# Two projection groups side by side, and smaller changes of order, loads and banks, in a hybrid attention block

## The chip, the cores and the metric

The kernel runs on one core of one Trainium2 chip. The metric is the device time of one execution in microseconds; the time before is the median of three runs.

## The reference

The block takes x (512 rows, 1024 columns, float32), normalises each row by its mean square, multiplies it by one wide input matrix, runs two attention branches of eight heads each on slices of the product, and merges them:

```python
h = rms_norm(x, norm_g)
proj = h @ w_in                      # 1024 x 6152
fq, fk, fv, fz, mq, mk, mv, mz, ga, gb, fl = split_cols(proj, IN_SPLITS)
log_f = log_sigmoid(fl + b_f)        # 8 columns
y_fox = fox_attention(rms_norm(fq), rms_norm(fk), fv, log_f) * silu(fz)
y_moba = moba_attention(rope(rms_norm(mq)), rope(rms_norm(mk)), mv) * silu(mz)
merged = sigmoid(ga + b0) * (y_fox @ w_fox) + sigmoid(gb + b1) * (y_moba @ w_moba)
out = x + merged @ w_out
```

## The kernel before, in words

Every product of two float32 matrices is made of three TensorE products of parts: each operand is split into a high part (a rounded copy) and a low part (what is left), and high x high, high x low and low x high are added up in PSUM. In the names, `wh_` and `wl_` are the parts of a weight, `Zh` and `Zl` those of x times norm_g (transposed, one tile of 128 x 512 for each of eight k), `Gh` and `Gl` those of the normalised x.

The matrix w_in is worked off in groups of 256 columns, named fqa, fka, fza and so on (a and b are the two halves of a slice). A group's weights come in two halves of four k each. The first two groups, fqa and fka (with the 8 columns of fl appended to fka), and the gates fza and fzb are multiplied by the parts Z, before the mean squares of the rows are known; later groups use G. `norm_row` turns the factors r of the rows into a tile (`rbc`) by four transposes on TensorE (tile `p_rbc`).

The start of the program: `first_loads` queues cst on ScalarE's queue and, on SyncE's, the pieces of fqa's weights (k 0, 1, 2 to 3, 4 to 7) between the eight tiles `xt` of x transposed. Eight products on a tile of zeros (`WARM`) run on TensorE meanwhile. `first_split` and `split_x` split what has landed; `load_fl` loads and splits fka's weights; `first_qk` multiplies all eight k of fqa into four PSUM banks (one for each 128 rows) and then all eight k of fka into the four others. `x_stats` loads x again by rows, in eight tiles of the tag "y" (15 buffers, eight of which hold `xt`), and sums the squares on ScalarE, with a scratch tile as output. `evac_qk` copies each bank to SBUF and normalises the heads.

Then come fza, fzb and fva, and four rounds of attention. `attn_group` gives the steps of a round of four heads: Tr (transposes and splits of q and k), Aa(h) (logits, minimum on VectorE, exponential on ScalarE), Bb(h) (transposes of the probabilities, products with v, sum into the tile `ypair`), Yp(pr) (product with the gate, split). The last step of a round, Yp(1), is run as `gate` inside the next round: before, behind that round's Aa(0). Projection groups are mixed in as filler. After that come the gate groups GA and GB, the products with w_moba, and the output product `group_o`, which makes a product of 2 x 2 blocks out of seven products of sums. `O_PRODUCTS` lists them with the number of the pair of PSUM banks that each is added into; `keep` copies banks to SBUF (`eo`) and adds x to them by a DMA from GpSimd, `result` adds a bank and a kept tile on VectorE (`ot`) and stores the sum.

PSUM has eight banks, in tags: "pj" 2, "tp" 3, "lg" 2, "pv" 1. The order of the instructions on each engine is set when the program is built, by a scheduler with modelled times that starts from the order of the text; on the chip each engine goes through its list in that order.

The order around the change, before:

```python
first_split(0, ((0,), (1, 2), (3, 4)))
first_split(1, ((5, 6), (7,)))
nc.sync.dma_start(out=wfl, in_=w_fl)
load_fl("fka", COLS["fka"], 0)
load_fl("fka", COLS["fka"], 1)
b1 = first_qk("fqa", (("pj", 2), ("pj", 2), ("lg", 2), ("lg", 2)))
b2 = first_qk("fka", (("tp", 3), ("tp", 3), ("tp", 3), ("pv", 1)))
```

Of the kernel before, what the change touches and what calls it, by code (L numbers as in the profile page):

```python
# [22 lines left out]
WARM = 8  # L23
# [6 lines left out]
def fox_moba_kernel(ctx: ExitStack, tc, xT, x, w_in, w_fl, w_fox, w_moba, w_out, cst, rope, out):  # L30
# [31 lines left out]

    XT, RAW = {}, {}

    def first_loads():
        def xt(eng, k):
            XT[k] = t2("y", 15, f"xt{k}")
            eng.dma_start(out=XT[k], in_=xT[:, k, :])

        def w(k0, k1):  # L70
            hf = k0 // 4
            if hf not in RAW:
                RAW[hf] = sb.tile([P, 4, CW], F32, name=f"wr_fqa{hf}", tag="wr", bufs=WR)
            nc.sync.dma_start(out=RAW[hf][:, k0 - 4 * hf:k1 - 4 * hf], in_=w_in[0, :, k0:k1, :])
# [46 lines left out]
    def split_x(*ks):  # L121
        for k in ks:
            xt = XT[k]
            zh, zl = Z[k] = [stage["pool"].tile([P, S], F32R, name=f"Z{hl}{k}") for hl in "hl"]
            A.activation(zh, xt, AF.Copy, scale=col(C_NG + k))
            V.scalar_tensor_tensor(zl, xt, col(C_NG + k), zh.bitcast(F32), op0=OP.mult, op1=OP.subtract)
# [12 lines left out]
    def load_fl(name, c0, hf):  # L139
        raw = sb.tile([P, 4, CW], F32, name=f"wr_{name}{hf}", tag="qk", bufs=4)  # L140
        nc.sync.dma_start(out=raw, in_=w_in[c0 // CW, :, 4 * hf:4 * hf + 4, :])
        hi, lo = split(raw, CW, f"{name}{hf}")
        f = wfl[:, 4 * hf:4 * hf + 4, :]
        A.activation(hi[:, :, CW:264], f, AF.Copy)
        V.tensor_tensor(out=lo[:, :, CW:264], in0=f, in1=hi[:, :, CW:264].bitcast(F32), op=OP.subtract)
        chunks.setdefault(name, []).append((hi, lo))

    def first_split(hf, between):
        raw = RAW[hf]
        hi = sb.tile([P, 4, 264], F32R, name=f"wh_fqa{hf}", tag="wh", bufs=4)  # L150
        lo = sb.tile([P, 4, 264], F32R, name=f"wl_fqa{hf}", tag="wl", bufs=4)
        for q, xs in enumerate(between):
            k = slice(2 * q, 2 * q + 2) if hf else slice(max(q, 2 * q - 2), max(q + 1, 2 * q))
            if hf == 0 and q < 2:
                V.tensor_copy(hi[:, k, :CW], raw[:, k])
            else:
                A.activation(hi[:, k, :CW], raw[:, k], AF.Copy)
            V.tensor_tensor(out=lo[:, k, :CW], in0=raw[:, k], in1=hi[:, k, :CW].bitcast(F32), op=OP.subtract)
            split_x(*xs)
        chunks.setdefault("fqa", []).append((hi, lo))  # L160

    COLS = {}
    off = 0
    for nm in ("fq", "fk", "fv", "fz", "mq", "mk", "mv", "mz"):
        for hfn in ("a", "b"):
            COLS[nm + hfn] = off
            off += CW
    for nm in ("ga", "gb"):
        for i in range(4):
            COLS[f"{nm}{i}"] = off  # L170
            off += CW
# [695 lines left out]
    def group_o():  # L867
# [74 lines left out]
        def keep(at, tq, cq):  # L942

            e[at] = sb.tile([P, 2, S], F32, name=f"eo{at}", tag="qk", bufs=4)
            for t in range(2):
                A.activation(e[at][:, t, :], b[at][t], AF.Copy)
                t0 = tq * HT + t * P
                G.dma_start(out=e[at][:, t, :], in_=x[t0:t0 + P, cq * 512:(cq + 1) * 512], accum_op=OP.add)
# [270 lines left out]
```

## Time and profile before

| | us |
|---|---|
| median of three runs | 426.72 (426.54 to 426.73) |
| the profiled execution, its own time | 427.16 |
| its span | 425.3 |
| TensorE busy | 418.5 |
| VectorE busy | 327.2 |
| ScalarE busy | 271.4 |
| GpSimd busy | 98.4 |

The span runs from the first to the last instruction of the profiled execution. A busy time counts an instruction's whole length. A line of the timeline gives start, length, engine, source line, operation, output and inputs; what stands in brackets is the idle time of that engine before it and what ended it.

### The profile page before, as it was taken

The numbers are of one execution on the slowest core, as the hardware profiler recorded it, in microseconds if no ns is written. First come the engines' busy times: TensorE is split into PE (matmuls) and PEld (weight loads), VectorE is DVE, ScalarE is ACT, GpSimd is POOL, SyncE is SP. The second block draws the span as 40 slices with busy tenths as digits, with TensorE's granted clock in tenths as the row PEclk, the third lists the DMA queues.
The fourth block names the chain that finished last, engine by engine and source line by source line (L and its number), as shares of the span: only waits on it lengthen the run. The fifth ranks groups of instructions, "written<-read, shape, count | busy, mean of one in ns | idle before, by whom it ended". The sixth has DMA issues, their size and how long they took to land.

```text
span 425.3 us, 7669 instructions
## 1 busy us (share of the span) xinstructions
PE 418.5 (98%) x2887; PEld 387.7 (91%) x2887; DVE 327.2 (77%) x570; ACT 271.4 (64%) x514; POOL 98.4 (23%) x120
## 2 busy tenths in 40 slices
PE   7999999999999999999999999999999999999996
PEld 6998899999999998899998878899999989988884
DVE  5669976769979769568767698767979698689973
ACT  4975436776868867568746687655656535686450
POOL 1048200225132850025750102140000000022140
PEclk9999999999999999999999999999999999999999
DMA  7981144235576334304124222463052603696484
GB/s 243 398 308 55 52 146 139 58 124 175 168 221 217 85 99 125 96 29 125 38 88 124 79 70 72 201 225 123 25 176 65 229 5 112 220 245 116 99 140 158
DMA packets 25621, 58.21 MB, mean 137 GB/s; under 512 B 3064, under 2 KB 7856, under 8 KB 25584
## 3 DMA queue, kind: packets, MB, share of 16 engines
q1 hardware_dynamic: 13392, 38.11, 27.3%
q10 hardware_dynamic: 8800, 11.21, 8.7%
q0 software_dynamic: 3392, 8.39, 8.5%
q8 instruction: 23, 0.38, 0.3%
q14 instruction: 14, 0.11, 0.1%
HBM read 48.11 MB, written 6.32 MB: 128 GB/s over the span
## 4 chain that ended last, share of the span: by engine, by line
PE 96%; DVE 2%; DMA 1%; issue 0%; ACT 0%; SPq 0%; DVEq 0%; ACTq 0%
PE pb_GB L753 3%; PE pb_GA L753 3%; PE pb_GB L750 3%; PE pb_GA L750 3%; PE pb_GB L752 3%; PE pb_GA L752 3%; PE po L939 3%; PE po L938 3%; PE po L940 3%; PE pv L611 2%; PE pv L610 2%; PE lg L556 2%; PE lg L555 2%; PE pm L681 2%; PE pm L680 2%; PE pm L679 2%
## 5 line engine op out<-in xcount | busy, mean ns | idle before, releaser
L560 ACT ACTIVATE p<-p,negm 128x128 f32<-128x128 f32 (+1 forms) x64 | 35.7, 559 | 9.8 <-DVE negm L558 8.6
L558 DVE CUSTOM_DVE_ANT_0 p<-lg,mask 128x128 f32<-128x128 f32 (+1 forms) x64 | 30.9, 485 | 14.3 <-PE lg L556 13.7
L334 POOL TENSOR_TENSOR ff<-ss,mh 128x8 f32<-128x8 f32 x16 | 26.7, 1678 | 65.2 <-DVE ss L332 64.7
L888 POOL DMA_DIRECT2D wr_o<-in_w_out_dram x4 | 4.9, 1293 | 95.5 <-ACT wr_o L887 95.5
L136 DVE TENSOR_TENSOR wl_GA<-wr_ga,wh_GA 128x1024 fp32r<-128x1024 f32 x14 | 17.8, 1288 | 5.8 <-ACT wh_GA L134 3.7
L901 ACT ACTIVATE wh_o<-wr_o 128x1024 fp32r<-128x1024 f32 x14 | 14.8, 1059 | 10.0 <-PE pb_GB L752 2.8
L134 ACT ACTIVATE wh_GB<-wr_gb 128x1024 fp32r<-128x1024 f32 x14 | 14.6, 1059 | 9.5 <-PE pm L680 3.5
L134 ACT ACTIVATE wh_GA<-wr_ga 128x1024 fp32r<-128x1024 f32 x14 | 14.6, 1059 | 9.3 <-PE pb_GA L752 4.6
L555 PE MATMUL lg<-KH,QS 128*128 128x128 f32 (+1 forms) x64 | 20.5, 329 | 0.0
L902 DVE TENSOR_TENSOR wl_o<-wr_o,wh_o 128x1024 fp32r<-128x1024 f32 x14 | 16.9, 1221 | 3.8 <-ACT wh_o L901 3.8
L136 DVE TENSOR_TENSOR wl_GB<-wr_gb,wh_GB 128x1024 fp32r<-128x1024 f32 x14 | 16.9, 1222 | 3.5 <-ACT wh_GB L134 3.5
L636 DVE TENSOR_TENSOR ypair<-pv,ysh 64x512 f32<-64x512 f32 x16 | 11.0, 688 | 11.0 <-ACT ysh L635 10.8
L607 DVE TENSOR_TENSOR ptl<-p_a,pth 128x512 fp32r<-128x512 f32 x16 | 11.0, 685 | 4.6 <-ACT pth L606 4.5
L529 DVE SCALAR_TENSOR_TENSOR QS<-p_qT,cs,QS 64x512 fp32r<-64x512 f32 x16 | 12.0, 750 | 2.5 <-ACT QS L528 2.1
L635 ACT ACTIVATE ysh<-pv 64x512 f32<-64x512 f32 x16 | 9.5, 593 | 6.7 <-PE pv L611 5.6
L753 PE MATMUL pb_GA<-Gh,wl_GA 128*128 128x256 f32 x48 | 13.6, 283 | 0.0
L752 PE MATMUL pb_GA<-Gl,wh_GA 128*128 128x256 f32 x48 | 13.5, 281 | 0.0
L750 PE MATMUL pb_GA<-Gh,wh_GA 128*128 128x256 f32 x48 | 13.5, 281 | 0.0
L753 PE MATMUL pb_GB<-Gh,wl_GB 128*128 128x256 f32 x48 | 13.5, 281 | 0.0
L752 PE MATMUL pb_GB<-Gl,wh_GB 128*128 128x256 f32 x48 | 13.4, 281 | 0.0
L679 PE MATMUL pf<-yhf,wh_wf 128*128 128x512 f32 x32 | 13.1, 408 | 0.4 <-DVE zs_mzb L425 0.4
L528 ACT ACTIVATE QS<-p_qT,cs 64x512 fp32r<-64x512 f32 x16 | 10.9, 681 | 3.8 <-PE lg L555 2.0
(458 smaller groups left out, 1785.9 us busy)
## 6 DMA issues: line engine op xcount, KB each, us to landing
wr_ga<-in_w_in_dram SPq DMA_DIRECT2D x8, 512.0 KB, 3.7
wr_gb<-in_w_in_dram SPq DMA_DIRECT2D x8, 512.0 KB, 5.1
wr_o<-in_w_out_dram SPq DMA_DIRECT2D x8, 512.0 KB, 5.1
xt<-in_xT_dram SPq DMA_DIRECT2D x8, 256.0 KB
x<-in_x_dram SPq DMA_DIRECT2D x8, 256.0 KB, 6.3
KH<-KH ACTq DMA_DIRECT2D x16, 128.0 KB, 2.4
s_dramh<-sum_sh ACTq DMA_DIRECT2D x8, 256.0 KB
s_draml<-sum_sl ACTq DMA_DIRECT2D x8, 256.0 KB, 3.6
```

The lines of the kernel that those rows point to most:

```text
L134: A.activation(hi[:, :, 0:n], src, AF.Copy)
L136: eng.tensor_tensor(out=lo[:, q, 0:n], in0=src[:, q], in1=hi[:, q, 0:n].bitcast(F32), op=OP.subtract)
L334: G.tensor_tensor(out=f2, in0=ss.rearrange("p t h -> p (t h)"), in1=mh, op=OP.pow)
L555: T.matmul(lg[:, :n], qs[:, qt], kh[:, :n], start=True, stop=False)
L558: V.tensor_tensor_reduce(pt, lg[:, :n], mask[:, 512 - n:512], -0.125, 3.0e38, op0=OP.add, op1=OP.min, accum_out=mkn[:, hh, i:i + 1])
L560: A.activation(pt, pt, AF.Exp, bias=mkn[:, hh, i:i + 1], scale=-1.0, accum_out=rs[:, hh, i:i + 1])
L679: T.matmul(p, hi[:, k, cc], yh, start=(k == 0), stop=False)
L750: T.matmul(o, hi[:, k, cc], lh, start=(n < 3 and c == 0 and k == 0), stop=False, skip_group_check=True)
L752: T.matmul(o, hi[:, k, cc], ll, start=False, stop=False, skip_group_check=True)
L753: T.matmul(o, lo[:, k, cc], lh, start=False, stop=(k == 3), skip_group_check=True)
L901: A.activation(wide(hi), wide(R[key, c]), AF.Copy)
L902: V.tensor_tensor(out=wide(lo), in0=wide(R[key, c]), in1=wide(hi).bitcast(F32), op=OP.subtract)
```

## The change

The first two groups are multiplied side by side: for each k first fqa's twelve products, then fka's, into all eight banks. The weights of fka are loaded in the same pieces as those of fqa, between the tiles of x, and `wfl` is loaded at the start on ScalarE's queue. The first tile of x comes in two halves, and is split in two halves. One warming product is left out. The last two tiles of `x_stats` get buffers of the tag "u", and the squares are written over their input. `norm_row` comes ahead of fka's evacuation. Yp(1) of a round stands behind Aa(1) of the next one. The second half of bank pair 3 is made in two quarters of 256 columns, the second one in a third bank of the tag "tp".

```diff
-WARM = 8
+WARM = 7
...
     def first_loads():
...
+        def w(nm, k0, k1):
             hf = k0 // 4
+            if (nm, hf) not in RAW:
+                tag, bufs = ("wr", WR) if nm == "fqa" else ("qk", 4)
+                RAW[nm, hf] = sb.tile([P, 4, CW], F32, name=f"wr_{nm}{hf}", tag=tag, bufs=bufs)
...
+        def xt(k, c0=0, c1=S):
+            if k not in XT:
+                XT[k] = t2("y", 15, f"xt{k}")
+            nc.sync.dma_start(out=XT[k][:, c0:c1], in_=xT[:, k, c0:c1])
         nc.scalar.dma_start(out=cs, in_=cst)
-        w(0, 1)
-        xt(nc.sync, 0)
-        w(1, 2)
-        xt(nc.sync, 1)
-        w(2, 4)
-        xt(nc.sync, 2)
-        xt(nc.sync, 3)
-        w(4, 8)
-        for k in range(4, KT):
-            xt(nc.sync, k)
+        nc.scalar.dma_start(out=wfl, in_=w_fl)
+        w("fqa", 0, 1)
+        xt(0, 0, 256)
+        xt(0, 256, S)
+        w("fka", 0, 1)
+        w("fqa", 1, 2)
+        xt(1)
+        w("fka", 1, 2)
+        w("fqa", 2, 4)
+        xt(2)
+        w("fka", 2, 4)
+        xt(3)
+        w("fqa", 4, 8)
+        xt(4)
+        w("fka", 4, 8)
+        for k in range(5, KT):
+            xt(k)
...
+    def split_x(k, parts=1):
+        xt = XT[k]
+        Z[k] = [stage["pool"].tile([P, S], F32R, name=f"Z{hl}{k}") for hl in "hl"]
+        n = S // parts
+        for c in (slice(i * n, (i + 1) * n) for i in range(parts)):
+            zh, zl = (z[:, c] for z in Z[k])
+            A.activation(zh, xt[:, c], AF.Copy, scale=col(C_NG + k))
+            V.scalar_tensor_tensor(zl, xt[:, c], col(C_NG + k), zh.bitcast(F32), op0=OP.mult, op1=OP.subtract)
...
+    def first_split(nm, k0, k1, on_v=False):
+        hf = k0 // 4
+        if len(chunks.setdefault(nm, [])) == hf:
+            hi = sb.tile([P, 4, 264], F32R, name=f"wh_{nm}{hf}", tag="wh", bufs=4)
+            lo = sb.tile([P, 4, 264], F32R, name=f"wl_{nm}{hf}", tag="wl", bufs=4)
+            chunks[nm].append((hi, lo))
+            if nm == "fka":
+                f = wfl[:, 4 * hf:4 * hf + 4, :]
+                A.activation(hi[:, :, CW:264], f, AF.Copy)
+                V.tensor_tensor(out=lo[:, :, CW:264], in0=f, in1=hi[:, :, CW:264].bitcast(F32), op=OP.subtract)
...
+        if on_v:
+            V.tensor_copy(hi[:, k, :CW], raw[:, k])
+        else:
+            A.activation(hi[:, k, :CW], raw[:, k], AF.Copy)
+        V.tensor_tensor(out=lo[:, k, :CW], in0=raw[:, k], in1=hi[:, k, :CW].bitcast(F32), op=OP.subtract)
...
-                xt = t2("y", 15, f"x{t}{hf}")
+                xt = t2("u", 4, f"x{t}{hf}") if t == NT - 1 else t2("y", 15, f"x{t}{hf}")
                 nc.sync.dma_start(out=xt, in_=x[t * P:(t + 1) * P, hf * 512:(hf + 1) * 512])
-                j = t2("u", 4, "junk")
-                A.activation(j, xt, AF.Square, accum_out=ms2[:, t, hf:hf + 1])
+                A.activation(xt, xt, AF.Square, accum_out=ms2[:, t, hf:hf + 1])
...
-                    {1: (("lg", 2), ("lg", 2)), 2: (("tp", 3), ("tp", 3)), 3: (("pj", 2), ("pj", 2)),
+                    {1: (("lg", 2), ("lg", 2)), 2: (("tp", 3), ("tp", 3)), 3: (("pj", 2), ("pj", 2), ("tp", 3)),
...
-            for t in range(2):
-                o = b[at][t].rearrange("p (n c) -> p n c", n=2)
+            for t, c in ((0, slice(0, 2)),) + (((1, slice(0, 1)), (1, slice(1, 2))) if at == 3 else ((1, slice(0, 2)),)):
+                o = b[at][t + c.start].rearrange("p (n c) -> p n c", n=2)[:, 0:c.stop - c.start, :]
...
+                if at == 3 and t:
+                    for c in range(2):
+                        A.activation(e[at][:, t, c * CW:(c + 1) * CW], b[at][t + c][:, :CW], AF.Copy)
...
-                    V.tensor_tensor(out=o[:, c:c + n], in0=b[bb][t][:, c:c + n], in1=e[ee][:, t, c:c + n], op=OP.add)
+                    V.tensor_tensor(out=o[:, c:c + n], in0=b[bb][t + 1][:, :n] if c else b[bb][t][:, :n], in1=e[ee][:, t, c:c + n], op=OP.add)
...
+    banks = {nm: [pst(tg, n, f"{nm}_{i}") for i, (tg, n) in enumerate(tags)] for nm, tags in
+             (("fqa", (("pj", 2), ("pj", 2), ("lg", 2), ("lg", 2))), ("fka", (("tp", 3), ("tp", 3), ("tp", 3), ("pv", 1))))}
+    for k0, k1 in ((0, 1), (1, 2), (2, 4), (4, 8)):
+        first_split("fqa", k0, k1, k0 == 0)
+        for k in range(k0, k1):
+            split_x(k, 2 if k == 0 else 1)
+            if k == k0:
+                first_split("fka", k0, k1)
+            first_qk(banks, k)
+    b1, b2 = banks["fqa"], banks["fka"]
     x_stats()
     for t in range(NT):
         evac_qk(b1[t], "fqa", t)
+    norm_row()
     for t in range(NT):
         evac_qk(b2[t], "fka", t)
     forget_exp()
-    norm_row()
...
-            body, tail = nxt[1][:1] + gate + nxt[1][1:], nxt[2]
+            at = 2
+            body, tail = nxt[1][:at] + gate + nxt[1][at:], nxt[2]
```

More of the change, by code (lines that the diff above doesn't have):

```diff
@@ L119, in fox_moba_kernel @@
     Z = {}
[L121 to L126, printed above, removed]
+    def split_x(k, parts=1):
[6 more added lines that the diff above has]
+            V.scalar_tensor_tensor(zl, xt[:, c], col(C_NG + k), zh.bitcast(F32), op0=OP.mult, op1=OP.subtract)
     chunks = {}
@@ L137, in split @@
         return hi, lo
[L139 to L160, printed above, removed]
@@ L372, in do_rope, with first_qk @@
         G.tensor_tensor(out=qn[:, :, :, 0:16], in0=ra, in1=rb, op=OP.add)
-    def first_qk(name, tags):
-        banks = [pst(tg, n, f"{name}_{i}") for i, (tg, n) in enumerate(tags)]
-        n = 264 if name == "fka" else CW
-        for kk in range(KT):
+    def first_qk(banks, kk):
+        for name, bank in banks.items():
+            n = 264 if name == "fka" else CW
             hi, lo = chunks[name][kk // 4]
@@ L1028, in seq @@
             u()
-    first_split(0, ((0,), (1, 2), (3, 4)))
-    first_split(1, ((5, 6), (7,)))
-    nc.sync.dma_start(out=wfl, in_=w_fl)
-    load_fl("fka", COLS["fka"], 0)
-    load_fl("fka", COLS["fka"], 1)
-    b1 = first_qk("fqa", (("pj", 2), ("pj", 2), ("lg", 2), ("lg", 2)))
-    b2 = first_qk("fka", (("tp", 3), ("tp", 3), ("tp", 3), ("pv", 1)))
+    banks = {nm: [pst(tg, n, f"{nm}_{i}") for i, (tg, n) in enumerate(tags)] for nm, tags in
[8 more added lines that the diff above has]
+    b1, b2 = banks["fqa"], banks["fka"]
     x_stats()
```

48 lines of the change are left out of this document (23 added, 25 removed).

## The prediction

> **What bounds the kernel now.** I read the page's head first, then the waits of TensorE.
>
> ```profile
> span 425.3 us, 7669 instructions
> PE 418.5 (98%) x2887; PEld 387.7 (91%) x2887; DVE 327.2 (77%) x570; ACT 271.4 (64%) x514; POOL 98.4 (23%) x120
> PE 96%; DVE 2%; DMA 1%; issue 0%; ACT 0%; SPq 0%; DVEq 0%; ACTq 0%
> ...
> PE warm_ps L107 <- DVE fg_pre L471: 1.5, 1, 1.5
> PE fqa L382 <- ACT Zh L125: 0.7, 1, 0.7
> PE pf L679 <- DVE zs_mzb L425: 0.4, 1, 0.4
> PE p_b L600 <- DVE ptl L607: 0.2, 1, 0.2
> ```
>
> The first line is the span, the second busy time by engine, the third the shares of the chain that ended last. The last four are all that PE waited for, with total, times and longest in us. PE is the chain, and between its first real product and its last it waits 0.6 us. So the change can win only in three places: before the first product, in that 0.6 us, and after the last product. Or it wins by making the products themselves quicker. Everything else matters only if it makes PE wait anew. The timeline of the start and the chain there:
>
> ```profile
> 0.80 0.40 SPq L74 DMA_DIRECT2D wr_fqa<-in_w_in_dram  x1
> 1.26 0.41 SPq L68 DMA_DIRECT2D xt<-in_xT_dram  x1
> 1.55 3.78 PE L107 MATMUL warm_ps<-warm 128*128 128x512 f32 x8 [1.55 <-DVE fg_pre L471]
> 3.64 0.29 DVE L155 CAST wh_fqa<-wr_fqa 128x256 fp32r<-128x256 f32 x1 [2.14 <-DMA wr_fqa<-in_w_in_dram]
> 5.27 0.72 ACT L125 ACTIVATE Zh<-xt,cs 128x512 fp32r<-128x512 f32 x1 [2.52 <-DMA xt<-in_xT_dram]
> 6.04 0.58 PE L382 MATMUL fqa<-wh_fqa,Zh 128*128 128x256 f32 x1 [0.71 <-ACT Zh L125]
> ...
> 9.19 0.21 PE fqa L383
> 9.77 0.12 PE fqa L382
> ```
>
> The columns of the first six are start, length, instruction; the bracket is the idle time before and its releaser. The first product needs the whole of xt 0 (256 KB) to land at 5.2 and then 0.72 us of ScalarE. The last two lines are steps of the chain: one product takes 0.21 until 9.4 and 0.12 from 9.8. The windows say it in sums:
>
> ```profile
> 3.00:4.00 1.00, 1.00 (x4) 0.81 (x3) 0.32 (x2) 0.00 (x0) 0.00 (x0) 1.00 0.84 179
> 6.04:9.40 3.36, 3.36 (x15) 3.36 (x16) 3.06 (x6) 2.46 (x4) 0.00 (x0) 1.00 1.03 357
> 9.80:19.10 9.30, 9.30 (x81) 9.30 (x81) 7.24 (x11) 8.10 (x17) 0.00 (x0) 1.00 1.05 396
> ```
>
> The second number is PE's busy time with its count of products, the last but two the granted clock, the last the GB/s. 15 products in 3.36 us are 0.224 each, 81 in 9.30 are 0.115. The granted clock reads 1.00 in both, so it does not show this slow stretch; the steps do. It costs about 15 x 0.109 = 1.6 us.
>
> **The change, part by part.**
>
> **Start.** The first xt comes as two DMAs of 128 KB, and the first product needs only the first half. Bounds for its landing: the equal-sized wr_fqa, issued 0.46 earlier, was used at 3.64, so not before 4.10; at the latest 5.27 as now. Half of the bytes between 3.64 and 5.27 gives 4.46. wfl (32 KB, moved from behind the x loads to ScalarE's queue ahead of this) adds 32 KB at the 179 GB/s above, 0.18: 4.64. Then half an activation, bounded by 0.72 and by an equal-sized copy, 0.38:
>
> ```profile
> L313 ACT ACTIVATE qn_fqa<-fqa x4: 373/384/385, 18.2 to 19.7; 128x256 f32<-128x256 f32 x4
> ```
>
> I take 0.50. With 0.05 of passing on, the first product starts at 5.2, in bounds of 4.6 to 6.0: **0.85 gained** (0.05 to 1.4). The warm-up is one product shorter, 7/8 of 3.78 us, so it ends near 4.9 and is not in the way. wfl's issue takes some 0.4 us of ScalarE's queue before its first work; ScalarE idles 2.52 us before Zh now, which hides it. I assume that the slow stretch moves along with the first product.
>
> Side by side, each k gives PE 24 products, 24 x 0.115 = 2.8 us of work (5.4 in the slow stretch). It needs 512 KB, 1.3 us at 396 GB/s; ScalarE needs 0.72 and two splits of at most 0.38, 1.5 us; the splits of wfl, which come at k = 0 and k = 4 now, stand behind Zh and have those 2.8 us too. So after k = 0 the supply is twice as fast as the use. The price of this order alone is nothing, since PE was not waiting for either group. Without that cover every us of lateness would be one of the total.
>
> **Hand-over.** Now fqa and fka hold all eight banks until the end of the loop.
>
> ```profile
> 19.20 1.07 SPq L226 DMA_DIRECT2D x<-in_x_dram  x1
> 27.46 0.63 ACT L228 ACTIVATE junk<-x 128x512 f32<-128x512 f32 x1 [1.02 <-DMA x<-in_x_dram]
> 28.97 1.04 POOL L232 TENSOR_TENSOR r<-mm,mh 128x4 f32<-128x4 f32 x1
> 30.75 0.39 PE L405 MATMUL pz_fza<-Zh,wh_fza 128*128 128x512 f32 x1
> 35.65 0.60 PE L240 MATMUL p_rbc<-ident,r 128*128 128x128 f32 x4
> ```
>
> The loop's end moves with its start, to 30.75 - 0.85 = 29.9. pz_fza needs the bank of fqa row 0. Its last product lies 21 products before the end, 2.4 us, and the copy is 0.38. p_rbc now comes ahead in the program, so it needs r by about 29.9 instead of 35.65. The eighth load of x was issued at 19.20, behind the weight loads, for want of a buffer; with tiles of their own all eight go out together, and r (ready at 30.0 now) comes some us sooner. The squares in place save nothing on the path. I cost this part at nothing; if r came no sooner, PE would wait about 0.1.
>
> **Middle.** Yp(1) of the old group is moved behind Aa(1) of the new one: one product and one round-off subtraction on VectorE, one copy on ScalarE, one product on POOL, at three group changes. Only the last of these changes shows PE waiting:
>
> ```profile
> 245.05 0.50 PE L679 MATMUL pf<-yhf,wh_wf 128*128 128x512 f32 x1 [0.37 <-DVE zs_mzb L425]
> 245.39 0.69 DVE L662 TENSOR_TENSOR ypair<-ypair,rinv_bc 128x512 f32<-128x512 f32 x1
> 248.16 0.67 DVE L607 TENSOR_TENSOR ptl<-p_a,pth 128x512 fp32r<-128x512 f32 x1
> 248.76 0.67 DVE L664 TENSOR_TENSOR ylm<-ypair,yhm 128x512 fp32r<-128x512 f32 x1
> 248.98 0.63 PE L600 MATMUL p_b<-ident,p 128*128 128x128 f32 x4 [0.19 <-DVE ptl L607]
> ```
>
> L662 is ahead of the late ptl on VectorE, so moving it takes up to 0.19 away; the wait of 0.37 ended before L662 began, so it stays. **0.1 gained** (0.19 gained to 1.4 lost at each change, the two VectorE steps in PE's way).
>
> **Last products.** In the two products of bank 3 (S3 and A22) 24 products of 512 columns become 48 of 256, the second quarter into a third bank.
>
> ```profile
> 399.56 1.28 DVE L956 TENSOR_TENSOR ot<-po,eo 128x512 f32<-128x512 f32 x2
> 404.67 1.08 ACT L946 ACTIVATE eo<-po 128x512 f32<-128x512 f32 x2
> ...
> 421.15 0.24 PE po L940
> 421.41 0.76 DVE L956 TENSOR_TENSOR ot<-po,eo 128x256 f32<-128x256 f32 x2 [1.39 <-PE po L940]
> 422.20 0.36 SPq L958 DMA_DIRECT2D out_dram<-ot  x1
> 422.50:423.00 0.50, 0.00 (x0) 0.00 (x0) 0.00 (x0) 0.00 (x0) 0.00 (x0) 1.00 0.53 178
> 423.00:423.50 0.50, 0.00 (x0) 0.00 (x0) 0.00 (x0) 0.00 (x0) 0.00 (x0) 1.00 0.98 332
> 423.50:424.00 0.50, 0.00 (x0) 0.00 (x0) 0.00 (x0) 0.00 (x0) 0.00 (x0) 1.00 0.05 14
> ```
>
> Two of 0.115 against one step of 0.24: **0.05 lost** at most. The third bank comes from the tag that the first result (L956 at 399.56) sets free; its chunk is the last third of a product kept at 404.67, so about 3 us of cover. One copy more on ScalarE, 0.16, is beside PE. At the end only one half-row add follows the last product instead of two: 0.76 - 0.42 = 0.34, the second add. The store that goes last also moves alone: 128 KB instead of 256 KB at 332 GB/s, up to 0.38 less, of which the earlier issue of the first half already gave part. I take **0.45 gained** (0.34 to 0.7).
>
> **Sum.** -0.85 - 0.1 + 0.05 - 0.45 = -1.35. On the profiled execution's 427.16 (span 425.3 and 1.9 around it) that is 425.8; the median, 426.72, lies 0.44 below that execution, so 425.4. This is 0.3%; a measurement of this kernel can tell 0.2%, 0.85 us, from no change.
>
> **The rivals.** *The slow stretch ends early.* The 0.71 us of idle ahead of the first product may be what makes the warm-up count for nothing: PE was busy from 1.55 to 5.33 and the products were still slow at 9.19. With the first product at 5.2 the idle shrinks to 0.3. Then most of the 1.6 us of slowness goes as well: another 0.8 to 1.6, 423.8 to 424.6. Against it: no row shows that so short a gap does not count.
>
> *The slow stretch ends when it ends.* If 9.6 is fixed to the start of the execution, the 0.85 us gained are spent at half rate and give 0.42: 425.8. For it: the times of three runs lie within 0.19 us, so the moment does not wander. [...]
>
> *Slower: VectorE at the group changes.* Yp(1) lands now next to Tr(1) and Bb(0), whose VectorE steps (QS, KL, ptl) PE needs at once.
>
> ```profile
> 80.00:120.00 40.00, 40.00 (x327) 39.38 (x326) 34.89 (x75) 30.73 (x67) 12.80 (x9) 1.00 0.49 148
> ```
>
> VectorE is the engine behind both late waits, and is busy 34.89 of 40 us in the first of these stretches. Price: 0.69 + 0.67 = 1.36 at a change, 4.1 for three; it decides above 2.2, or 0.73 at each. Two of three: 428.1. Against: the first two changes show no wait now, with projection products to fill.
>
> *The halves release nothing.* If the first product still waits for both halves, the two activations of 0.5 replace 0.72: 0.28 lost instead of 0.85 gained, 426.5. Against: the CAST at 3.64 ran while later pieces of the same tile were still to land.
>
> **How the numbers follow.** Forecast 0.45; early end of the slow stretch 0.20; fixed end 0.15; slower 0.12; halves 0.08. The forecast's own range is 424.8 to 425.9. The range takes in the early end below (423.9) and the halves above (426.8); outside lie the slower case and a corner of the first rival. Faster by over 0.2% (below 425.87): 0.38 of the forecast, 0.20, and 0.06 of the fixed end, 0.64. Same: 0.07 + 0.09 + 0.07 = 0.23. Slower: 0.13.
>
> **What would show it.** Right: the first L382 near 5.2; 0.21 steps for some 3.4 us after it; no PE wait between 5.2 and the end except that on zs_mzb; one 256-column L956 after the last product; PE's last product some 0.9 us sooner than 421.4. Wrong: steps of 0.12 already at 7 or still 0.21 at 9.4 (the clock rivals), PE waiting on p_rbc or pz_fza near 30, or new waits on VectorE at the three group changes.

## The result: slower by 0.9%

| | before | changed |
|---|---|---|
| median, us | 426.73 (6 runs) | 431.06 (6 runs, 429.78 to 431.77) |
| the profiled execution, its own time | 427.16 | 431.69 |
| its span | 425.3 | 429.7 |

The ratio of the runs is 1.0094, interval 1.0083 to 1.0106. The forecast was 425.4 with a range of 423.9 to 426.8: the direction was wrong, and the result lies 4.3 us above the range. One execution of experiment 2 took 454.20 us at a granted clock of 0.852 and is left out of the medians below.

The head of the changed kernel's page, and then all that PE waited for (total, times, longest in us):

```profile
span 429.7 us, 7707 instructions
PE 419.4 (98%) x2910; PEld 389.5 (91%) x2910; DVE 329.2 (77%) x571; ACT 270.8 (63%) x518; POOL 110.4 (26%) x120
```
```profile
PE lg L561 <- DMA KH<-KH: 2.1, 1, 2.1
PE pj_fva L314 <- DVE v_fva L352: 2.0, 1, 2.0
PE warm_ps L128 <- DVE fg_pre L477: 1.5, 1, 1.5
PE pj_mqa L314 <- DVE v_fvb L352: 1.0, 1, 1.0
PE pf L685 <- DVE zs_mzb L431: 0.3, 1, 0.3
```

The waits ahead of p_b (0.2) and of the first fqa product (0.7) are gone, as the prediction said. Three new ones, 5.1 us together, have come. Two of them stand at projection products (fva, mqa) that the change does not touch. The timeline gives their places; the first line is the start of the real products:

```profile
4.17 0.51 ACT L148 ACTIVATE Zh<-xt,cs 128x256 fp32r<-128x256 f32 x1 [0.95 <-DMA xt<-in_xT_dram]
4.73 0.58 PE L389 MATMUL fqa<-wh_fqa,Zh 128*128 128x256 f32 x1
6.82 0.41 PE L390 MATMUL fqa<-wl_fqa,Zh 128*128 128x256 f32 x1
8.11 0.28 PE L391 MATMUL fka<-wh_fka,Zl 128*128 128x264 f32 x1
8.23 0.28 PE L390 MATMUL fka<-wl_fka,Zh 128*128 128x264 f32 x1
...
59.06 0.42 DVE L352 TENSOR_TENSOR v_fva<-pj_fva,v_fva 128x256 fp32r<-128x256 f32 x1
59.53 0.39 PE L314 MATMUL pj_fva<-wh_fva,Gh 128*128 128x256 f32 x1 [2.03 <-DVE v_fva L352]
114.37 0.36 PE L314 MATMUL pj_mqa<-wh_mqa,Gh 128*128 128x256 f32 x1 [0.97 <-DVE v_fvb L352]
122.60 0.33 PE L561 MATMUL lg<-KH,QS 128*128 128x128 f32 x1 [2.10 <-DMA KH<-KH]
```

The start works better than forecast: the first product comes at 4.73, and the steps are 0.12 from about 8 on. At 28.99 PE begins pz_fza, 1.76 us ahead of before (30.75). At 59.5 all of that lead is gone. Before, the same pair of rows was as follows, with PE's product ahead of the second one between them:

```profile
58.70 0.42 DVE L344 TENSOR_TENSOR v_fva<-pj_fva,v_fva 128x256 fp32r<-128x256 f32 x1
59.03 0.28 PE L308 MATMUL pj_fva<-wh_fva,Gl 128*128 128x256 f32 x1
59.17 0.39 PE L306 MATMUL pj_fva<-wh_fva,Gh 128*128 128x256 f32 x1
```

The bank of fva's third unit comes free with this copy. Before, PE's product starts 0.05 us after the copy's end (58.70 + 0.42 = 59.12) and the list of waits shows nothing. The 0.05 is no room: in the changed kernel, where PE stands and waits, its product also starts 0.05 after the copy's end (59.48). Its length of 0.39 is that of the product behind the wait, too; its neighbours take 0.28. So PE had nothing to spare here already before the change. The windows over three stretches, before and then changed (after the engine PE the columns are PEld, DVE, ACT, POOL, each busy time and count, then granted clock):

```profile
31.00:60.00 29.00, 29.00 (x155) 24.64 (x154) 27.86 (x56) 14.87 (x24) 13.21 (x14) 1.00 0.28 90
60.00:104.00 44.00, 44.00 (x365) 43.51 (x364) 31.22 (x72) 29.22 (x64) 10.42 (x7) 1.00 0.38 111
104.00:124.00 20.00, 20.00 (x165) 19.78 (x165) 19.20 (x42) 15.13 (x31) 3.94 (x3) 1.00 0.67 215
```
```profile
31.00:60.00 29.00, 26.97 (x145) 22.85 (x143) 28.70 (x55) 15.02 (x26) 19.34 (x16) 1.00 0.33 113
60.00:104.00 44.00, 44.00 (x367) 43.53 (x366) 29.23 (x74) 27.80 (x63) 7.87 (x5) 1.00 0.37 110
104.00:124.00 20.00, 16.92 (x134) 16.23 (x134) 19.71 (x41) 12.85 (x27) 6.36 (x5) 0.99 0.54 168
```

VectorE was busy 27.86 of 29 us between 31 and 60 already before, and 19.20 of 20 between 104 and 124. In these two stretches PE and VectorE are both full, and the new waits lie at the end of the first and inside the second. In finer windows the clock behind the last wait:

```profile
120.00:124.00 4.00, 1.90 (x14) 1.59 (x13) 3.87 (x10) 1.65 (x5) 0.00 (x0) 0.95 1.05 343
124.00:128.00 4.00, 4.00 (x23) 3.72 (x22) 3.40 (x10) 3.05 (x9) 0.00 (x0) 0.63 0.33 115
128.00:132.00 4.00, 4.00 (x36) 4.00 (x36) 0.99 (x3) 1.75 (x4) 1.64 (x1) 1.00 0.71 189
```

The granted clock is 0.63 in the 4 us behind the wait, with 23 products in them, and 1.00 in the next 4, with 36; mqa's products begin 0.21 us apart from 125.04 to 126.74, and 0.12 from 127.10 on. Priced by the clock that is 4 x 0.37 + 4 x 0.05 = 1.7 us, an estimate. The bill from the profiled executions: start -1.76; waits +2.03, +0.97, +2.10; clock +1.7; p_b and pf -0.3; tail -0.68 (3.63 from the last product's start to the end, 4.31 before); outside the span +0.13. That is +4.2 of the +4.5 measured; 0.3 is not placed.

### The profile page after: what moved, and what is told of

The parts are those of the page before. It is cut to its first block, busy times and chain, and to the rows that moved or that the text cites. A ratio compares the mean times of both kernels' runs of the same rounds, so it can differ in the third digit from the quotient of the medians.

```text
span 429.7 us, 7707 instructions
## 1 busy us (share of the span) xinstructions
PE 419.4 (98%) x2910; PEld 389.5 (91%) x2910; DVE 329.2 (77%) x571; ACT 270.8 (63%) x518; POOL 110.4 (26%) x120
## 4 chain that ended last, share of the span: by engine, by line
PE 70%; DVE 2%; DMA 1%; ACT 1%; issue 0%
PE pb_GB L759 3%; PE pb_GA L759 3%; PE pb_GA L756 3%; PE pb_GB L756 3%; PE pb_GB L758 3%; PE pb_GA L758 3%; PE po L947 3%; PE po L946 3%; PE po L945 3%; PE pv L617 2%; PE pv L616 2%; PE pf L685 2%; PE pm L687 2%; PE pf L687 2%; PE pf L686 2%; PE pm L686 2%
## 5 line engine op out<-in xcount | busy, mean ns | idle before, releaser
L342 POOL TENSOR_TENSOR ff<-ss,mh 128x8 f32<-128x8 f32 x16 | 30.1, 1885 | 74.4 <-DVE ss L340 46.9
L159 DVE TENSOR_TENSOR wl_GA<-wr_ga,wh_GA 128x1024 fp32r<-128x1024 f32 x14 | 16.9, 1224 | 4.6 <-ACT wh_GA L157 3.9
L561 PEld LDWEIGHTS lg<-KH,QS 128*128 128x128 f32 x64 | 12.1, 189 | 3.2 <-DMA KH<-KH 2.4
L756 PE MATMUL pb_GB<-Gh,wh_GB 128*128 128x256 f32 x48 | 13.3, 281 | 0.0
```

The source lines that it names most:

```text
L159: eng.tensor_tensor(out=lo[:, q, 0:n], in0=src[:, q], in1=hi[:, q, 0:n].bitcast(F32), op=OP.subtract)
L342: G.tensor_tensor(out=f2, in0=ss.rearrange("p t h -> p (t h)"), in1=mh, op=OP.pow)
L561: T.matmul(lg[:, :n], qs[:, qt], kh[:, :n], start=True, stop=False)
L756: T.matmul(o, hi[:, k, cc], lh, start=(n < 3 and c == 0 and k == 0), stop=False, skip_group_check=True)
```

## The experiments

The medians are in us. The kernel before had 426.8 to 427.0 in these comparisons; its profile, and that of the changed kernel, are those above. The waits are PE's behind 50 us, pf's wait near 245 to 250 left out.

| | kernel | median | ratio to before | PE's waits |
|---|---|---|---|---|
| 1 | changed, old squares | 432.47 | 1.0117 (1.0099 to 1.0135) | v_fva 2.1, v_fvb 1.9 |
| 2 | changed, Yp(1) back | 431.3 | 1.0111 (1.0093 to 1.0129) | v_fva 2.1, KH 0.9, qn_mqa 0.3, ptl 0.2 |
| 3 | changed, groups one after the other | 427.49 | 1.0016 (1.0001 to 1.0031) | none |
| 4 | before, start alone | 433.22 | 1.0134 (1.0116 to 1.0153) | v_fva 2.4, v_fvb 2.0, ptl 0.2 |
| 5 | before, halves alone | 431.55 | 1.0127 (1.0091 to 1.0162) | v_fva 0.9, v_fvb 1.8, ptl 0.2 |
| 6 | changed, copies first | 424.43 | 0.9939 (0.9924 to 0.9955) | v_fva 0.8 |
| 7 | before, load on VectorE | 432.09 | 1.0112 (1.0092 to 1.0133) | v_fva 2.0, sums 0.8, ptl 0.2, v_mva 0.2 |
| 8 | before, tail alone | 426.92 | 0.9992 (0.9983 to 1.0001) | ptl 0.2 |
| 9 | before, attention later | 427.40 | 1.0008 (0.9998 to 1.0019) | v_fva 0.5, ptl 0.2 |
| 10 | as 6 | 424.73 | 0.9947 (0.9929 to 0.9964) | v_fva 0.6 |
| 11 | before, copies first | 426.73 | 0.9995 (0.9982 to 1.0007) | ptl 0.2 |
| 12 | 6 and gates later | 427.59 | 1.0012 (0.9995 to 1.0029) | KH 2.2 |
| 13 | changed, stores on SyncE | 431.13 | 1.0082 (1.0050 to 1.0113) | v_fva 2.5, sums 1.1, v_fvb 0.4 |
| 14 | 6 and stores on SyncE | 425.51 | 0.9966 (0.9954 to 0.9978) | v_fva 0.2 |
| 15 | 12 and stores on SyncE | 429.08 | 1.0040 (1.0020 to 1.0059) | v_fva 1.0, KH 1.2 |
| 16 | 3 and copies first | 427.07 | 1.0001 (0.9992 to 1.0011) | none |
| 17 | changed, sums later | 432.70 | 1.0151 (1.0133 to 1.0168) | v_fva 1.7, then three of 0.3 to 1.2 at 178 to 183 |
| 18 | 6 and Yp(1) back | 425.97 | 0.9980 (0.9968 to 0.9992) | v_fva 0.5, KH 0.3, ptl 0.2 |

### Which part of the change costs (1 to 4)

**1.** The tile lines of `x_stats` as before:

```diff
-                xt = t2("u", 4, f"x{t}{hf}") if t == NT - 1 else t2("y", 15, f"x{t}{hf}")
+                xt = t2("y", 15, f"x{t}{hf}")
...
-                A.activation(xt, xt, AF.Square, accum_out=ms2[:, t, hf:hf + 1])
+                j = t2("u", 4, "junk")
+                A.activation(j, xt, AF.Square, accum_out=ms2[:, t, hf:hf + 1])
```

> The changed kernel with one part undone: the tiles of x for the mean squares come all eight from the tag y again, with a scratch tile for the squares. Theory A (early mean squares): with tiles of their own, r is ready sooner, so the scheduler's list for VectorE has the eight normalising steps ahead of fka's statistics and of the forget chain; that delays the copies of fva, p_LR and the first logits. Undone, VectorE's list has them in the order of before, the 2.0 us wait of PE at 57 to 59 goes, p_LR comes near 65.5 instead of 71.3, and as the late attention is what runs the filler dry, the waits at 114 and 120 go as well: 424.5 to 426.0. Theory B (Yp(1) moved): only the 2.0 us go, 428.5 to 429.5. Theory C (side by side bunches the evacuations of both groups behind 29 us): nothing changes, 430.5 to 431.5.

Measured 432.47, a wait of 2.1 at the same place. Theory A, my first one, is refuted: p_rbc comes at 36.8 instead of 31.1 and VectorE's list has the order of before, but fva's first copy still comes at 59.58 and the first logits at 78.3.

**2.** Yp(1) where it was:

```diff
-            at = 2
+            at = 1
```

> The changed kernel with one part undone: Yp(1) stands behind Aa(0) of the next round again. Theory B: the waits of 1.0 and 2.1 us at 114 and 120 go, and the fall of the granted clock behind them: 426.0 to 428.0. Theory A: the first logits are as late as before (78.7), the filler is used up as early, and PE waits at the first group change for another releaser: 429.5 to 431.5, and the 2.0 us wait on fva's copies stays. Theory C as A.

431.3: no gain. Theory B is refuted; the same 2.1 on fva, and the later wait is smaller (0.9) but there.

**3.** The products of fqa first, then those of fka, and the loads in that order:

```diff
-            if k == k0:
-                first_split("fka", k0, k1)
-            first_qk(banks, k)
+            first_qk({"fqa": banks["fqa"]}, k)
+    for hf in range(2):
+        first_split("fka", 4 * hf, 4 * hf + 4)
+        for k in range(4 * hf, 4 * hf + 4):
+            first_qk({"fka": banks["fka"]}, k)
```

> The changed kernel with one part undone: fqa's eight k first, then fka's, with the weights loaded in the order of before; the halves of the first x tile, seven warming products and the early load of wfl stay. Theory C: fqa's statistics run beside fka's products again, VectorE has 2 to 3 us less to do behind 31, and PE's wait at 57 to 59 is under 0.5: 425.0 to 428.0. Theory A: the normalising steps still stand ahead of fka's statistics in VectorE's list, the wait stays at 1.5 to 2.5 and the logits at 77 to 79: 429.5 to 432.0. Both expect the first product near 4.7 and steps of 0.12 from about 7.7 as in the changed kernel.

427.49, no wait at 59. That looks like theory C, but the profile gives another reason, PE's wait at the start:

```profile
PE fqa L386 <- ACT Zh L145: 2.0, 2, 1.4
```

One group alone uses x twice as fast, PE waits 2.0 us for it and reaches fva at 54.49, later than before (53.49). VectorE's first copy comes at 58.77, about as before. PE is not early there, so it does not wait.

**4.** The changed kernel with the squares, the norm row, Yp(1) and the last products all as before (the hunks of the last products and of experiment 1 taken back too):

```diff
-    norm_row()
     for t in range(NT):
         evac_qk(b2[t], "fka", t)
     forget_exp()
+    norm_row()
...
-            at = 2
+            at = 1
```

> The kernel before with the start alone changed: halves of the first x tile, seven warming products, wfl early, both groups side by side; the mean squares, the place of the norm row, Yp(1) and the last products as before. Theory A and B: the start's gain of 1.8 us (first product at 4.7, slow stretch over at 7.7) reaches the end but for what VectorE takes back at 57 to 59, where PE came only 0.1 us behind it before: 425.0 to 426.5. If VectorE takes all of it back: 426.7. Theory C: waits as in the changed kernel, 429.0 to 431.5.

433.22: the start alone costs all of the loss and more. PE reaches fva at 51.04 (51.68 in the changed kernel), the copy comes at 58.78. My 425.0 to 426.5 took for granted that only the wait itself would be lost.

### VectorE between 31 and 60 (5 to 8, 11, 16)

**5.** Before, with the first x tile in halves, seven warming products and wfl early:

```diff
-        xt(nc.sync, 0)
+        XT[0] = t2("y", 15, "xt0")
+        for c in (slice(0, 256), slice(256, S)):
+            nc.sync.dma_start(out=XT[0][:, c], in_=xT[:, 0, c])
```

> The kernel before with the first x tile in halves, wfl loaded early and seven warming products, and nothing else: fqa and fka one after the other. Theory D (VectorE is the bound up to 59 us): in the first four experiments and both first kernels VectorE makes fva's first copy at 58.7 to 59.6, whether PE reached fva at 51.0 or at 54.5, so what the start gains PE waits away there. In this kernel's list one gate step of 0.63 stands behind that copy instead of ahead, so the copy comes near 58.2 and is done at 58.5; PE, 1.3 to 1.8 us sooner, is there at 57.4 to 57.9 and waits 0.6 to 1.1 on fva's copies; 425.8 to 426.8. Theory C (side by side itself): no wait there, the whole start gain reaches the end, 425.0 to 425.5.

431.55, a miss on both sides. The two groups end no sooner (31.17; 30.91 before), as PE waits 1.9 us for Zh and Zl at the start. The norm row comes 1.4 us later (37.05), VectorE's copy comes at 59.94, 1.2 later, and PE waits 0.9 there and 1.8 near 116:

```profile
PE pj_mqa L311 <- DVE v_fvb L349: 1.8, 1, 1.8
PE pj_fva L311 <- DVE v_fva L349: 0.9, 1, 0.9
```

No group stands side by side here, so a loss of this kind does not need it. In the changed kernel theory C can explain little of the wait: its copy is only 0.36 us later than before (59.06, 58.70), while PE reaches fva 1.8 us sooner. Here VectorE is 1.2 us late at 59, and the time is 4.5 us longer.

**6.** The splits of fqb's weights, which the scheduler had put ahead of fva's first copy, are tied behind its second one:

```diff
+                def do():
+                    chunks.setdefault(name, []).append(split(raw[0], CW, ...))
+                if name == "fqb":
+                    with tc.issue_after(FVA[1]):
+                        do()
...
-    seq(["fva"])
+    AHEAD[0] = 1
+    seq(["fva"])
+    AHEAD[0] = 3
```

(`FVA` holds the last VectorE instruction of each unit of fva; `AHEAD` is the look-ahead of `pump`, 3 before.)

> The changed kernel with one thing added: the splits of fqb's weights (two steps of 1.22 us on VectorE) stand behind fva's second copy in VectorE's list instead of ahead of the first one. Theory D: fva's first copy comes near 56.7 instead of 59.1, PE's wait of 2.0 us there is under 0.2, the forget chain is done sooner, p_LR comes near 67 and the first logits near 74; the waits at 114 and 120 and the fall of the clock go as well: 424.0 to 426.0. Theory C: the wait at 57 to 59 goes but the round of attention is as late as before, and the waits at 114 to 122 stay: 427.5 to 429.5. If the wait at 59 is only moved to fqb's weights, 429 to 431.

In the changed kernel these two steps of VectorE were:

```profile
54.72 1.22 DVE L159 TENSOR_TENSOR wl_fqb<-wr_fqb,wh_fqb 128x1024 fp32r<-128x1024 f32 x1
56.55 1.22 DVE L159 TENSOR_TENSOR wl_fqb<-wr_fqb,wh_fqb 128x1024 fp32r<-128x1024 f32 x1
```

424.43: 6.6 us below the changed kernel and 0.61% below the kernel before, the fastest of all. VectorE's copy, PE behind it, and PE's waits:

```profile
57.82 0.41 DVE L360 TENSOR_TENSOR v_fva<-pj_fva,v_fva 128x256 fp32r<-128x256 f32 x1
58.29 0.39 PE L322 MATMUL pj_fva<-wh_fva,Gh 128*128 128x256 f32 x1 [0.76 <-DVE v_fva L360]
```
```profile
PE pj_fva L322 <- DVE v_fva L360: 0.8, 1, 0.8
PE pf L695 <- DVE zs_mzb L441: 0.3, 1, 0.3
```

The copy came 1.2 us sooner and not 2.4: in this execution VectorE's list ran 0.6 later already at the second split of fva (49.95, 49.38 changed), and small steps moved into the gap. So a wait of 0.8 was left. The first logits come at 71.83 (78.73 changed, 72.76 before), and nothing waits from 60 to 240. The one edit makes VectorE free sooner at 58 to 60, and the scheduler then also puts p_LR behind 9 products of fqb instead of the changed kernel's 47. This run does not separate the two; experiments 9 and 17 bear on the second.

**7.** The reverse, in the kernel before: five steps of VectorE that change no value.

```diff
+        if name == "fva" and t == 0:
+            for z in (ZS["f", 0], ZS["f", 1], ZS["f", 0], ZS["f", 1], ZS["f", 0]):
+                V.tensor_tensor(out=z, in0=z, in1=z, op=OP.max)
```

> The kernel before with five needless steps of 128x512 on VectorE (a gate tile against itself, maximum, 0.64 us each), four of them ahead of fva's first copy, which changes no value. Theory D: the copy comes at about 60.4, PE waits 1.3 to 1.9 us for it at 59.2, and the time is longer by that and by what the granted clock loses behind it (0 to 1.8 us): 428.0 to 430.5. If VectorE had room there: 426.5 to 427.2.

432.09, 5 us longer.

```profile
59.99 0.41 DVE L347 TENSOR_TENSOR v_fva<-pj_fva,v_fva 128x256 fp32r<-128x256 f32 x1
60.45 0.39 PE L306 MATMUL pj_fva<-wh_fva,Gh 128*128 128x256 f32 x1 [2.03 <-DVE v_fva L347]
```

The copy is 1.3 us later than before and PE waits 2.0; it had reached fva 0.9 us sooner in this execution (52.60, 53.49 before). Experiments 6 and 7 together show the cause of the first loss: VectorE's list sets the time at 59. In the profiles of 1 to 4, 8, 9 and both first kernels the copy comes between 58.3 and 59.6, whether PE reaches fva at 51.0 or at 54.5. The loss of 5 us, above my 430.5, is once more larger than the delay of the copy, 1.3, and than PE's wait, 2.03.

**8.** The tail alone, the diff's hunks of `product`, `keep` and `result` put into the kernel before.

> The kernel before with the last products alone changed (second half of bank pair 3 in two quarters, the second one in a third bank). The prediction's term is 0.4 gained: 426.3 to 426.7 beside 427.0; the profile of the changed kernel (0.68 less between the last product and the end) says 0.5 to 0.7. No theory of the middle expects anything else; a gain under 0.1 would say that the 48 small products eat it.

-0.34 us (-0.73 to +0.04) by the interval: it agrees with the 0.4 of the prediction, and is too small to be told from nothing.

**11.** The edit of 6 in the kernel before.

> The kernel before with the splits of fqb behind fva's second copy, nothing else. Theory D: PE arrives at fva's third unit 0.1 us behind the copy already, so to free VectorE there gives nothing by itself: 426.6 to 427.2, and the 2.6 us that this edit and the changed kernel together have gained are the start's 1.8, the tail's and the wait of 0.19 on p_b. If the order of the splits is a gain of its own: 424.5 to 426.0.

426.73, the same as before: PE was not waiting there, so the order alone gives nothing. The gain of 6 is the start's lead let through.

**16.** The edit of 6 in the kernel of 3.

> The third experiment (fqa first, then fka) with fva's copies ahead of the splits of fqb. PE reaches fva at 54.5 there, later than in the kernel before, and has no wait on the copies, so theory D says no gain: 426.4 to 427.6. If side by side is not what lets the start gain through, but the order of the splits is: 424.5 to 425.5.

427.07. PE waits 2.3 us for Zh at the start and reaches fva at 55.45. So the start's gain needs both: two groups side by side, so that x may come at half the rate, and VectorE's copies sooner.

### The second loss, 104 to 124 (9, 10, 12 to 15, 17, 18)

**9.** The changed kernel has 47 products of fqb ahead of p_LR in TensorE's list, before there are 14, and its first logits come 6 us later. Here the kernel before has p_LR and the first Tr written behind the first fqb unit:

```diff
-    head[0]()
+    early = filler(plan[0][4])[:1]
+    for u in early:
+        u()
+    forget_lr()
+    head[0]()
```

> The kernel before with the transposes to LR and the first Tr written behind the first fqb unit instead of ahead of it. VectorE's list up to fva's copies is that of before; in TensorE's list the first logits stand behind 72 products of fqb instead of 48. Theory E (the place of the first attention round in TensorE's list decides the later loss): there is no wait at 59, but the first logits come near 76 and PE waits 1 to 2 us near 115 on fvb's copies, as in the start alone and the halves alone: 429.0 to 431.5. Theory D without E (only VectorE's lateness at 59 and the clock behind it cost): 426.6 to 427.4.

427.40. The first logits come 2.5 us later (75.24) and cost nothing, so theory E is refuted as far as this goes: p_LR moved only 0.8 us here, not the changed kernel's 4.3, and the edit brought 24 products of fqb ahead of it, not 47.

**13.** KH's DMA stood behind stores of the sums in ScalarE's queue (its ACTIVATE at 119.67, the DMA's issue at 121.06):

```diff
-                A.dma_start(out=d, in_=t)
+                nc.sync.dma_start(out=d, in_=t)
```

> The changed kernel with the stores of the sums issued from SyncE's queue instead of ScalarE's. Theory F (the later waits come from KH's DMA, which stands behind two stores in ScalarE's queue at 119.5 to 121.1): KH's DMA is issued near 119.8, the wait of 2.1 us of the logits near 121 falls under 0.8 and the clock stays up behind it: 427.5 to 429.5. Theory G (VectorE, slowed beside GpSimd at 106 to 112, is late as a whole there): another wait of 1 to 3 us takes its place, 430.0 to 431.5. Both: the wait of 2.0 on fva's copy stays.

431.13, nothing gained.

```profile
PE pj_fva L314 <- DVE v_fva L352: 2.5, 1, 2.5
...
PE lg L561 <- DMA s_dramh<-sum_sh: 1.1, 1, 1.1
PE pf L685 <- DVE zs_mzb L431: 0.9, 1, 0.9
PE pj_mqa L314 <- DVE v_fvb L352: 0.4, 1, 0.4
```

KH's DMA is now issued right behind its copy (120.94, the copy ends at 120.90), and the wait ahead of the logits falls from 2.1 to 1.1. But the copy itself comes 0.55 later (120.22), fva's wait is 0.5 longer and pf's 0.6, and the median stays. So the stores made a part of that one wait, and taking it away gained nothing: theory F's 427.5 to 429.5 is missed.

**17.** The sums of the output product, 3 us of VectorE each, moved from the first round to the second:

```diff
-        if n == 0:
+        if n == 1:
...
-                at = 3 * k + 5
+                at = 2 * k + 1
```

> The changed kernel with the four sums for the output product (3 us each on VectorE) made in the second attention round instead of the first, which takes some 9 to 12 us of VectorE's work out of 95 to 128 us. Theory G (VectorE is the bound from 104 to 124, and what it has not done by 104 is waited for: 29.2 us between 60 and 104 in the changed kernel, 31.2 before): the waits of 1.0 and 2.1 us at 113 to 122 and the lower clock behind them go, only the wait of 2.0 on fva's copies stays: 426.0 to 428.5. If the late first logits (78.7) cost PE for another reason than VectorE: 430.0 to 432.0.

432.70, but the place is what was asked:

```profile
104.00:124.00 20.00, 20.00 (x166) 19.77 (x165) 12.96 (x27) 12.30 (x26) 7.58 (x6) 1.00 0.30 83
164.00:184.00 20.00, 17.67 (x96) 14.43 (x95) 19.75 (x39) 15.00 (x31) 0.00 (x0) 1.00 0.60 179
```

With VectorE at 12.96 instead of 19.71 of 20, PE waits for nothing between 104 and 124, and mva's products begin at 143.68 (149.35 changed, 143.81 before). The first logits are late here too (78.3), and PE waits for nothing from 60 to 176: late logits by themselves make no wait. So theory G holds for this place, VectorE's work there is what the second loss needs; its time, 426.0 to 428.5, is missed. The work then fills VectorE at 164 to 184 (14.26 before), PE waits there and 1.6 us ahead of pf, and all is lost again. Why the median is higher still stays open.

A full VectorE is not enough for a wait, though. Experiment 3 has none, with this window:

```profile
104.00:124.00 20.00, 20.00 (x166) 19.71 (x165) 19.72 (x39) 13.33 (x25) 3.06 (x2) 1.00 0.74 215
```

Nor does the work done by 104 tell the two apart: from 60 to 104 VectorE was busy 30.57 us in experiment 3, without a wait, and 30.80 in experiment 5, with one of 1.8. Which step behind the first loss has to be late for the second to follow stays open.

**12, 15, 10, 14.** Tries at the 0.8 that experiment 6 left. 12: the last step of the fzb gates also behind fva's second copy.

```diff
+                if name == "fzb":
+                    LATE.append(gate_step)
...
+    with tc.issue_after(FVA[1]):
+        for u in LATE:
+            u()
```

> The changed kernel with fva's copies first, and also the last step of the two fzb gates (0.63 us each on VectorE) behind fva's second copy. The wait of 0.8 on fva's first copy goes: 423.2 to 424.4, 0.5 to 0.8 below the kernel with the copies first. If VectorE's next work (the splits of fqb) then comes too late: a wait on them near 64 and no gain.

427.59: the wait on fva goes, but the first logits now wait 2.2 us for KH at 73.9. 15 has the stores on SyncE as well; its expectation puts that wait near 120, where it was not:

> The kernel with fva's copies first and the fzb gates later, which waited 2.2 us near 120 on KH's DMA, with the stores on SyncE's queue. Theory F: that wait goes, 423.0 to 424.6, and the spread of 4 us between its runs shrinks to under 2. Theory G: a wait on VectorE takes its place, 426.5 to 428.5.

429.08; the wait on KH, at 73.6, shrinks to 1.2 and the one on fva is back. Neither theory spoke of that place, so this run decides nothing between them. 10 is the kernel of 6 unchanged:

> The changed kernel with fva's copies first, once more as it stands, as the partner of the next two runs: 423.9 to 425.2, PE's wait of 0.8 on fva's first copy, no wait between 60 and 240.

424.73. And 14, the kernel of 6 with the edit of 13:

> The changed kernel with fva's copies first and the stores of the sums on SyncE's queue. It has no wait between 60 and 240 to lose, so both theories say 423.9 to 425.2 as with the copies first alone; above 426 would say that SyncE's loads of weights are held up by the stores.

425.51: no wait over 0.4, and still 1.1 us above 6 and 0.8 above 10. The interval overlaps that of 10 (0.9954 to 0.9978, 0.9929 to 0.9964) and the profiled spans are the same (423.1), so a difference to that kernel is not shown.

**18.** The kernel of 6 with the edit of 2.

> The changed kernel with fva's copies first and Yp(1) behind Aa(0) as before. The prediction gave Yp(1)'s move 0.1 (the wait of 0.19 on p_b): 424.4 to 425.0 beside 424.4 with the copies first, and a wait on p_b near 248 again. Over 426 would say that the move of Yp(1) is a large part of what the copies-first kernel gains.

425.97, 1.5 us above 6 and 1.2 above 10. Without the two losses the move of Yp(1) gains more than my 0.1: p_b's wait of 0.18 is back, as the prediction had it, and 0.3 on KH at 72; the rest of the 1.5 has no row of its own.

## Why the prediction was wrong, point by point

**What bounds the kernel.** "Everything else matters only if it makes PE wait anew." That sentence is right; the step that failed is the sum, which does not follow it: it counts the 0.85 us won at the first product whole at the end and puts all that lies between at 0.1 gained. The ground for that was a list with only 0.6 us of waits. A list of waits shows where PE is late, not how near it is to waiting. VectorE's copy at 59 left PE no room at all, at the end of 29 us in which VectorE was busy 27.86; the prediction read no window of VectorE there. What the runs showed in its place: the start's 1.76 is waited away at 59 (2.03), and 0.97 and 2.10 of waits and 1.7 of lower clock follow. Experiments 6 and 7 show that this copy's time is VectorE's own.

**Start.** Mis-sized, and in the good direction: 0.85 forecast, 1.31 at the first product (4.73), 1.76 at the end of the two groups. The half landed by 4.17 and not 4.64; the half activation was 0.51 (0.50). The slow stretch lasted 3.0 us (4.73 to 7.7) instead of 3.5 (6.04 to 9.6), which is near the assumption that it moves along with the first product. The first rival's case, most of the slowness gone and steps of 0.12 at 7, did not come: the step at 6.82 is still 0.21. Its reason, the 0.71 of idle, is contradicted by the changed kernel: there is no idle ahead of the first product (the last warming product ends at 4.90), and the steps are 0.21 all the same. But the end is not tied to the first product either: with first products at 4.76 and 4.83 it came near 6.1 in experiment 18 and 6.4 in experiment 16, and in experiment 15, with 4.79, the steps are 0.12 from 5.10 on. So that the two agreed here was luck. I had said of a fixed end that the three runs within 0.19 us show a moment that does not wander; these ends do wander. The times can be steady all the same if VectorE takes such differences back at 59. That fits experiment 9, whose start is that of the kernel before: PE reaches fva at 52.50 there (53.49 before) and waits 0.5. Experiment 8, with the same start, reaches it at 52.91 and shows no such wait (PE busy 28.99 of the 29 us from 31 to 60). No run tests it by itself.

**Hand-over.** "I cost this part at nothing." For the bank and r that was right: PE has no wait on pz_fza or p_rbc. The cover that was not named was VectorE's.

**Middle.** The wait on p_b went, as forecast. The bound of 1.4 lost at each change was weighed for Yp(1) alone. The loss at the first group change (3.1 of waits, 1.7 of clock) was outside it, and it was not Yp(1)'s: with Yp(1) put back, experiment 2 gains nothing that can be told and experiment 18 loses.

**Last products.** As forecast, as far as it can be told: 0.4 gained by the sum's two terms, -0.34 (-0.73 to +0.04) in experiment 8, and one half-row add of 0.42 as the last:

```profile
426.39 0.42 DVE L967 TENSOR_TENSOR ot<-po,eo 128x256 f32<-128x256 f32 x1 [0.88 <-PE po L947]
```

**The rivals.** The slower one named the right engine, VectorE, and the wrong work and place: steps that the change moves, at the group changes. The work that counted is not moved at all. What moved was PE, to a time at which VectorE had not finished. "VectorE steps in PE's way" should have been asked of every stretch that PE would reach sooner.

**The order of the lists.** The prediction took the lists of the engines as fixed but for the edited lines. The scheduler made them anew: p_LR stands behind 47 products of fqb instead of 14, and the first logits come 6 us later. Experiment 9 shows that 2.5 of these alone cost nothing, and in experiment 17 the 5.5 us cost no wait before 176.

## What to carry to other kernels

Before you count a gain at the front, follow PE's lead to the next place where another engine is also full: there the later of the two sets the time, and a list of waits that shows nothing may hide that there is no room left. Look for the step that PE needs and see what stands ahead of it on that engine without haste. Here two splits of 1.22 us did, at 54.7 to 57.8, for products that begin at 65.8; putting them behind the copy turned a loss of 4.3 us into a gain of 2.6.

## What the runs showed of the hardware

**Behind some waits of 2 us the granted clock was lower.** Behind a wait of 2.1 at 60 in experiment 1 it was 0.57 for 4 us, with 20 products in them and 36 in the next 4. Priced by the clock that is 4 x 0.43 = 1.7 us more, an estimate:

```profile
60.00:64.00 4.00, 3.95 (x20) 3.96 (x21) 2.09 (x11) 0.00 (x0) 0.00 (x0) 0.57 0.45 154
64.00:68.00 4.00, 4.00 (x36) 4.00 (x35) 1.53 (x7) 1.47 (x3) 0.00 (x0) 1.00 0.00 0
```

Behind a wait as long at the same place in the changed kernel (60 to 64, 36 products) and in experiment 7 (60 to 104) the clock stayed at 1.00. The runs of experiment 15 fall in two groups by it: 426.8 to 427.8 where the clock of the whole run was 0.999 or 1.0 (5 runs), 428.8 to 430.8 where it was 0.995 or 0.996 (7 runs); the profiled execution, of 426.95, is in the first group. 0.4% of 430 is 1.7 us, one such stretch by the same estimate. This can be a part of why kernels with such waits spread over 2 to 4 us, but not all: the groups lie further apart than 1.7, and the changed kernel has a run of 431.54 at 1.0 and one of 430.57 at 0.995. The clock was lower behind 2.1 and 1.9 in experiment 1 (0.57 from 60 to 64, 0.91 from 104 to 124), 2.4 in experiment 4 (0.57 from 60 to 64), 2.1 in the changed kernel (0.63 from 124 to 128) and 2.2 in experiment 12 (0.70 from 75 to 79), and not behind 2.5 in experiment 13 (1.00 from 60 to 104). So the length of the wait alone does not tell the two cases apart; what does was not shown.

**Some steps of VectorE took longer while GpSimd's product ran.** In the changed kernel a split took 2.06 beside it and a subtraction of Gl 1.53; the other split of fva took 1.22, the other seven subtractions 0.63 to 0.68:

```profile
45.03 1.22 DVE L159 TENSOR_TENSOR wl_fva<-wr_fva,wh_fva 128x1024 fp32r<-128x1024 f32 x1
48.83 0.63 DVE L255 TENSOR_TENSOR Gl<-xt,Gh 128x512 fp32r<-128x512 f32 x1
48.91 3.43 POOL L344 TENSOR_TENSOR qn_fka<-qn_fka,ff 128x512 f32<-128x512 f32 x2
49.38 2.06 DVE L159 TENSOR_TENSOR wl_fva<-wr_fva,wh_fva 128x1024 fp32r<-128x1024 f32 x1
51.36 1.53 DVE L255 TENSOR_TENSOR Gl<-xt,Gh 128x512 fp32r<-128x512 f32 x1
```

No run here tests the reason. Between 31 and 60 four steps beside such products were longer (1.03, 1.53, 2.06 and 1.53), 3.3 us in all above the median length of their form; before there were three (0.83, 1.53, 1.53), 2.3 us. Experiments 14 and 18, with the copies first, have steps of 1.03, 2.06 and 1.53 there as well, so that is not what decides here.
